# A hybrid decoder layer in split precision on one core: the low-half subtraction of four down weights made in two halves

## The chip, the core and the metric

The kernel runs on one NeuronCore of a Trainium2 chip. TensorE multiplies, VectorE, ScalarE and GpSimd do the rest of the arithmetic, and SyncE issues the DMA transfers. The metric is the device time of one execution in microseconds (us), as the median of several runs. Where the text explains where time goes, it uses one profiled execution, whose own time stands beside the median below.

## The reference

The kernel computes one decoder layer for 1024 tokens of width 1024, with 16 learned meta tokens in front, in float32. Two feed-forward networks (ffn1 and ffn2) enclose a mixer of two kinds of heads:

```python
def swiglu(h, w_gate, w_up, w_down):
    return (jax.nn.silu(h @ w_gate) * (h @ w_up)) @ w_down
...
        n = rms_norm(h, ffn1_norm[l])
        h = h + 0.5 * swiglu(n, ffn1_w_gate[l], ffn1_w_up[l], ffn1_w_down[l])
        n = rms_norm(h, mix_norm[l])
        proj = n @ w_in[l]
...
        sb_out = stick_breaking_attention(q, k, v)
        rw_out = rwkv7_time_mix(proj[..., 3 * SB_WIDTH:], ...)
        h = h + jnp.concatenate([sb_out, rw_out], axis=-1) @ w_out[l]
        n = rms_norm(h, ffn2_norm[l])
        h = h + 0.5 * swiglu(n, ffn2_w_gate[l], ffn2_w_up[l], ffn2_w_down[l])
    return rms_norm(h, final_norm)[:, N_META:]
```

The feed-forward width d_ff is 2816, which is 22 blocks of 128. The change lies in the feed-forward networks alone.

## The kernel before

**Split products.** Each float32 operand x is split into a high part, xh = round(x), and a low part, xl = x - xh. A product is three matmuls that accumulate in one PSUM bank: high by high, high by low and low by high (`mm3`, L720). A weight tile arrives by DMA as `wraw` (128 partitions by 1024 float32, 512 KB). ScalarE copies it, rounded, into `whi`; VectorE then subtracts to get `wlo`. Both are one instruction per tile (`split`, L504; `wsplit`, L558). The tiles wraw, whi and wlo have two buffers each, so a new weight can be split only when the last but one has been multiplied.

**The order of the stages.** The 1040 rows are cut into two groups, A (the meta tokens and the first half) and B (the second half). TensorE's main stream runs ffn1 on A (stage 0), the input projections of A, ffn1 on B (stage 1), the projections of B, the output projection of A, ffn2 on A (stage 2), and ffn2 on B (stage 3). Beside this main stream the mixer's work (RWKV and attention) is put into the gaps of each engine's queue. Stages 1 and 2 have mixer work beside them; in them the products of the main stream take turns in two PSUM banks (`DB = 2`, L34).

**Inside a stage.** d_ff is walked in parts (`PARTS`, L52): a first part of two blocks, then parts of four. For each block the main stream makes the gate and up products (pg, pu), and the activation is split again into `ah` and `al`. Then come the down products of the part. One part of two blocks needs two down tiles, each 2 blocks deep by 512 output columns; one of four needs four tiles. Between the up product of the last block of a part and the down products stands the gate product of the next part's first block. A down product `pd` (L1066) covers one output block m of 128, with three matmuls for each block of d_ff in the part; when it is done, VectorE adds it to the residual:

```python
            self.mm3(pd, self.row(dh, j, mw * P)[:, ms], self.row(dl, j, mw * P)[:, ms], ah, al, i == 0, i == nf - 1)
        hd = h[:, m, c0:c1]
        with self.urgent():
            nc.vector.scalar_tensor_tensor(hd, pd, 0.5, hd, ALU.mult, ALU.add)
```

The profile calls that addition `h<-pd,h`. Only it frees the PSUM bank.

**What sets the order.** Every engine works through its queue in order, and the order is fixed when the program is built. A planner (`Clock`, L195) keeps a clock for each engine with a cost per instruction (`cost`, L273). `catch_up` (L391) takes, over all engines, the pending instruction that could start first; among equals the more urgent. Loads and splits of weights have the level "load", the residual's additions are "urgent", and an urgent one is taken if it is ready no more than 0.1 after the other (`AHEAD`, L49):

```python
                    key = (max(t, c, self.port if o.port else self.dma - BACKLOG if e == "s" else 0.0)
                           - AHEAD * (o.prio[0] == -self.URGENT), o.prio)
```

`o.port` marks instructions of VectorE that read two SBUF operands, and GpSimd's: the planner lets only one of these run at a time. VectorE's cost in it is 0.11 + 0.00111 per element of a partition (L281), a matmul's of this kind 0.4545e-3 per column and 0.001 more (L300, L314). When an instruction is issued, its clock advances, and everything that follows is placed by the new state.

The weights are loaded in the order that `plan` (L1369) yields them. `loads` (L568) issues the DMA as soon as a buffer of wraw is free, `splits` (L587) calls `wsplit` for each. A small function in `plan`, `laid` (L1429), sets for each weight how its rows are laid out in the tile. In stages 1 and 2 the first block of d_ff in a down tile of two blocks lies on one side of the tile, the second on the other, 512 elements each, with a gap.

Of the kernel before, what the change touches and what calls it, by code (L numbers as in the profile page):

```python
# [7 lines left out]
F32 = mybir.dt.float32  # L8
F32R = mybir.dt.float32r
I32 = mybir.dt.int32  # L10
AF = mybir.ActivationFunctionType
ALU = mybir.AluOpType
# [53 lines left out]
def quad_order(nm):  # L66

    parts, qf = FPARTS[nm], QF[nm]
    for i, (f0, f1) in enumerate(parts):
        if f0 >= qf:  # L70
            q, nd = 0, parts[i - 1][1] - parts[i - 1][0]
            for x in "d" * nd + ("gu gu" if f1 > f0 + 2 else "gu") if f0 == qf else "gdudd gdu" if nd == 4 else "gdu gdu":
                if x == " ":
                    f0 += 2
                elif x == "d":
                    yield x, parts[i - 1], q
                    q += 1
                else:
                    yield x, None, f0
# [16 lines left out]
class Eng:  # L96


    def __init__(self, real, name, clk):
        self._r, self._n, self._c = real, name, clk  # L100
# [381 lines left out]
class Ker:  # L482
    def __init__(self, tc, A, out):
        self.tc, self.A, self.out = tc, A, out
        self.clock, self.fast = Clock(), None
        self.wq, self.wr, self.cur, self.flags = [], [], (), {}
        self.lay, self.edge = None, False
        self.nc = NC(tc.nc, self.clock)
        self.need = self.clock.need
        self.after = lambda *aps: self.clock.need(*aps, slack=False)  # L490


    def two(self, *aps, bank):

        n = self.need(*aps, bank=bank)
        n.both = True
        return n
# [57 lines left out]
        by = w.shape[3] // nm  # L555
        return w[:, k // by // 2, k // by % 2, k % by * nm:(k % by + 1) * nm]

    def wsplit(self, raw, nk, nm, pool, lay):  # L558
        self.clock.ahead = True
        self.nsplit = getattr(self, "nsplit", 0) + 1  # L560
        hi, lo = self.wtiles(nk, nm, pool, lay)
        if len(hi.shape) > 3:
            raw = raw.rearrange("p k c -> p (k c)").rearrange("p (a b c) -> p a b c", b=2, c=hi.shape[3])
        self.split(hi, lo, raw, self.nc.gpsimd if self.nsplit < 3 else None)
        self.clock.ahead = False
        return hi, lo

    def loads(self, plan):  # L568

        for x in plan:  # L570
            if not isinstance(x, tuple):
                yield x
                continue
            raws, lay = [], self.lay
            if isinstance(x[0], tuple):
                for src, ring in zip(x[0], ((self.wp, "wr", 2), (self.fast.q, "wr2", 2))):
                    yield self.need(bank=ring)
                    raws.append(self.wraw(src, *x[1:3], ring))
                    self.hold(raws[-1:])
            else:  # L580
                yield self.need(bank=(self.wp, "wr", 2))
                raws.append(self.wraw(*x[:3]))
                self.hold(raws)
            self.wr.append((x, raws, lay))
        self.wr.append(None)

    def splits(self):  # L587

        while True:
            yield lambda: self.wr  # L590
            if self.wr[0] is None:
                return
            x, raws, lay = self.wr[0]
            if len(raws) == 2:
                self.wq.append((x, []))
                yield from self.pair(raws, self.wq[-1][1])
                self.drop(raws)
                self.wr.pop(0)
                continue
            raw, = raws  # L600
            pool = self.wx if len(x) > 3 else self.wp
            for tag in ("wh", "wl"):
                yield self.need(bank=(pool, tag, 2))
            self.wq.append((x, self.wsplit(raw, *x[1:3], pool, lay)))
            self.hold(self.wq[-1][1])
            self.drop((raw,))
            self.wr.pop(0)
# [761 lines left out]
    def plan(self):  # L1369

        F = self.flags
        cols = lambda name, c0, n: (self.wcols(name)[:, :, c0:c0 + n], KT, n)

        def proj(g, late):
            rw, sb = self.proj_items(g)
            for it in 2 * sb[-NL:] if late else rw + sb[:-NL]:
                yield cols("w_in", *it[:2])

        def wout(late):
            for m in WOUT[late]:  # L1380
                yield cols("w_out", m * P, P)

        def ffn(nm, poll=False, wx=False, fast=False, once=False):
            gu = lambda c, f: cols(nm + "_w_" + c, f * P, P)
            two = lambda c, f: ((gu(c, f)[0], gu(c, f + 1)[0]), KT, P)
            kept = lambda l: [x + (True,) * (i > 1) for i, x in enumerate(l)] if wx else 2 * l
            def down(f0, f1, q):
                dw = self.A[nm + "_w_down"][0].rearrange("(f p) m -> p f m", p=P)
                mw = KT // (f1 - f0) * P
                return dw[:, f0:f1, q * mw:q * mw + mw], f1 - f0, mw  # L1390
            qf = QF.get(nm, 0)
            for f0, f1 in FPARTS[nm] if fast else PARTS:
                if fast and f0 >= qf:
                    break
                if f0 == 0 and once:
                    yield from [gu(c, f) for f in range(f0, f1) for c in ("gate", "up")]
                elif f0 == 0:
                    yield from kept([gu(c, f) for f in range(f0, f1) for c in ("gate", "up")])
                else:
                    for f in range(f0, f1):  # L1400
                        if f > f0:
                            if poll and F.get("f2b") and "woutat" not in F:
                                F["woutat"] = f
                                yield from wout(True)
                            yield gu("gate", f)
                        yield gu("up", f)
                if fast and f1 >= qf:
                    continue
                if f1 < NFT:
                    if poll and F.get("f2b") and "woutat" not in F:  # L1410
                        F["woutat"] = f1
                        yield from wout(True)
                    yield gu("gate", f1)
                self.edge = f1 == NFT and not poll
                yield from [down(f0, f1, q) for q in range(f1 - f0)]
                self.edge = False
            for op, x, f in quad_order(nm) if fast else ():
                if op == "d":
                    yield down(*x, f)
                elif op == "u" and f == NFT - 2:  # L1420
                    yield from (gu("up", f), gu("up", f + 1))
                else:
                    yield lambda: self.fast
                    yield two("gate" if op == "g" else "up", f)
            if fast:
                self.edge = True
                yield from [down(*PARTS[-1], q) for q in range(4)]
                self.edge = False
        def laid(gen, stage):  # L1429
            for x in gen:  # L1430
                if isinstance(x, tuple):
                    src = x[0][0] if isinstance(x[0], tuple) else x[0]
                    self.lay = LAY.get((0 if self.edge else stage, next((n for n in ("down", "w_out") if n in src.name), "up")))
                yield x
        yield from laid(ffn("ffn1", wx=True, fast=True), 0)
        yield from laid(proj(0, False), 0)
        yield from laid(proj(0, True), 0)
        yield from laid(ffn("ffn1", once=True), 1)
        yield from laid(proj(1, False), 1)
        yield from laid(proj(1, True), 0)  # L1440
        yield from laid(wout(False), 1)
        yield from laid(ffn("ffn2", True), 2)
        if "woutat" not in F:
            yield lambda: F.get("f2b")
            F["woutat"] = None
            yield from laid(wout(False), 2)
        yield from laid(ffn("ffn2", wx=True, fast=True), 3)
# [650 lines left out]
    def attn(self, g, bufs, nw, ahead):  # L2098
# [23 lines left out]
        def worker():  # L2122
            while items:
# [9 lines left out]
                if not any(left.values()):  # L2133
                    F["attn", g] = True
        self.clock.spawn(loads(), 4)
        self.clock.spawn(zs(), 2)
        for i in range(nw):
# [556 lines left out]
```

## Time and profile before

| | |
|---|---|
| median of 3 runs | 2219.96 us (2219.08 to 2220.79) |
| the profiled execution | 2222.34 us |
| its span, first to last instruction | 2220.6 us |
| ScalarE busy (whole span) | 1097.1 us (49%) |
| split subtractions of weights, wlo on VectorE | 312, 412.6 us in all |
| additions of a down product to the residual of A or the first stages, `h<-pd,h` | 200, 107.0 us in all |

In the profile PE is TensorE's matmuls, PEld its weight loads, DVE is VectorE, ACT ScalarE, POOL GpSimd and SPq SyncE's queue of DMA issues. A row of the timeline gives the start, the duration, the engine, the line, the operation, output and inputs (out<-in), shapes, and, in brackets, how long the engine stood idle before it and what released it. Every instruction is recorded by one helper, so all rows carry L110; they are told apart by the names of their tiles. In this execution the first part of stage 1 has its down products at 610 to 625 us and that of stage 2 at 1351 to 1364 us.

### The profile page before, as it was taken

What the parts mean: (1) busy time and instruction counts of PE and PEld (TensorE: products, weight loads), DVE (VectorE), ACT (ScalarE), POOL (GpSimd) and SP (SyncE); (2) the same over time, 40 slices, a digit from 0 to 9 for tenths busy, and PEclk for the clock granted to TensorE, in tenths of its full rate; (3) what the DMA queues carried; (4) which work ended last, traced back from release to release, by engine and by line L of the source; (5) the groups of instructions that cost most, each with busy time, mean ns of one, the idle gap of its engine ahead of it and who ended that gap; (6) DMA issues with size and microseconds to landing.
All of it is one profiled execution on the core that took longest, in us unless ns stands there. A gap on an engine that the chain in (4) does not pass through costs nothing.

```text
span 2220.6 us, 41509 instructions
## 1 busy us (share of the span) xinstructions
PE 2192.2 (99%) x16304; PEld 1954.9 (88%) x16304; DVE 1549.7 (70%) x2632; ACT 1097.1 (49%) x2177; POOL 574.1 (26%) x723
## 2 busy tenths in 40 slices
PE   9999999999999999999999999999999999999998
PEld 8999999999878888888888987887878899899998
DVE  6887776475666655576576887556777756898774
ACT  6454444534444534565435564445666436455444
POOL 2321121013142231453012424314444101322120
PEclk9999999999999999999999999999999999999999
DMA  7533332645633232432556534234232343334332
GB/s 217 147 105 105 102 89 79 174 133 137 201 106 99 76 102 77 122 97 75 160 145 191 166 102 119 73 95 129 72 90 78 117 132 121 111 105 114 105 92 80
DMA packets 408745, 257.60 MB, mean 116 GB/s; under 512 B 45013, under 2 KB 392373, under 8 KB 408550
## 3 DMA queue, kind: packets, MB, share of 16 engines
q1 hardware_dynamic: 408550, 254.95, 39.8%
q8 instruction: 128, 2.10, 0.4%
q14 instruction: 67, 0.55, 0.1%
HBM read 220.90 MB, written 33.99 MB: 115 GB/s over the span
## 4 chain that ended last, share of the span: by engine, by line
PE 91%; DVE 3%; ACT 2%; issue 2%; DMA 1%; SPq 0%; POOL 0%; DVEq 0%; ACTq 0%; POOLq 0%
PE pd L110 33%; PE pu L110 21%; PE pg L110 20%; PE pwo L110 3%; PE px L110 3%; PE po L110 2%; PE pz L110 2%; PE pat L110 2%; DVE wlo L110 1%; PE pG L110 1%; ACT whi L110 1%; SPq L110 0%; PE pp L110 0%; PE psw L110 0%; PE pss L110 0%
## 5 line engine op out<-in xcount | busy, mean ns | idle before, releaser
L110 ACT ACTIVATE whi<-wraw 128x1024 fp32r<-128x1024 f32 x314 | 330.5, 1053 | 314.4 <-PE pd L110 195.0
L110 DVE TENSOR_TENSOR wlo<-wraw,whi 128x1024 fp32r<-128x1024 f32 (+1 forms) x312 | 412.6, 1324 | 91.8 <-ACT whi L110 87.1
L110 PE MATMUL pd<-ah,whi 128*128 128x512 f32 (+2 forms) x944 | 323.1, 342 | 4.1 <-DVE h L110 3.7
L110 PE MATMUL pd<-ah,wlo 128*128 128x512 f32 (+2 forms) x944 | 317.8, 337 | 0.0
L110 PE MATMUL pd<-al,whi 128*128 128x512 f32 (+2 forms) x944 | 316.9, 336 | 0.8 <-DVE al L110 0.8
L110 PE MATMUL pd<-nh,whi 128*128 128x256 f32 (+7 forms) x648 | 210.2, 324 | 0.2 <-DVE st L110 0.2
L110 PE MATMUL pu<-nh,whi 128*128 128x512 f32 (+3 forms) x576 | 205.6, 357 | 0.0
L110 PE MATMUL pd<-nh,wlo 128*128 128x256 f32 (+7 forms) x648 | 203.9, 315 | 0.0
L110 PE MATMUL pd<-nl,whi 128*128 128x256 f32 (+7 forms) x648 | 203.5, 314 | 0.0
L110 PEld LDWEIGHTS pd<-ah,whi 128*128 128x128 f32 x944 | 177.6, 188 | 24.4 <-DVE h L110 5.0
L110 PE MATMUL pu<-nh,wlo 128*128 128x512 f32 (+3 forms) x576 | 197.2, 342 | 0.0
L110 PE MATMUL pu<-nl,whi 128*128 128x512 f32 (+3 forms) x576 | 196.1, 340 | 0.0
L110 POOL TENSOR_TENSOR qs<-wraw 128x512 f32<-128x512 f32 x64 | 98.5, 1541 | 372.0 <-DVE ql L110 141.9
L110 PE MATMUL pg<-nh,whi 128*128 128x512 f32 (+3 forms) x536 | 194.4, 364 | 0.2 <-ACT whi L110 0.2
L110 PEld LDWEIGHTS pd<-ah,wlo 128*128 128x128 f32 x944 | 177.4, 188 | 19.2
L110 PEld LDWEIGHTS pd<-al,whi 128*128 128x128 f32 x944 | 177.6, 188 | 18.2 <-DVE al L110 1.5
L110 PE MATMUL pg<-nl,whi 128*128 128x512 f32 (+3 forms) x536 | 186.2, 349 | 0.0
L110 PE MATMUL pg<-nh,wlo 128*128 128x512 f32 (+3 forms) x536 | 185.5, 351 | 0.5 <-DVE wlo L110 0.5
L110 DVE SCALAR_TENSOR_TENSOR h<-pd,h 128x256 f32<-128x256 f32 (+1 forms) x200 | 107.0, 539 | 66.9 <-PE pd L110 66.0
L110 POOL TENSOR_TENSOR al<-sl,ah 128x512 fp32r<-128x512 f32 (+2 forms) x45 | 74.3, 1651 | 297.7 <-ACT ah L110 288.2
L110 PEld LDWEIGHTS pd<-nh,whi 128*128 128x128 f32 (+2 forms) x648 | 120.8, 186 | 12.0 <-issue 3.1
L110 PEld LDWEIGHTS pd<-nh,wlo 128*128 128x128 f32 (+2 forms) x648 | 120.5, 186 | 8.3
(413 smaller groups left out, 5609.4 us busy)
## 6 DMA issues: line engine op xcount, KB each, us to landing
wraw<-in_ffn_w_gate_dram SPq DMA_DIRECT2D x90, 512.0 KB
wraw<-in_ffn_w_up_dram SPq DMA_DIRECT2D x90, 512.0 KB
wraw<-in_ffn_w_down_dram SPq DMA_DIRECT2D x88, 512.0 KB
wraw<-in_w_in_dram SPq DMA_DIRECT2D x54, 512.0 KB
wraw<-in_w_out_dram SPq DMA_DIRECT2D x20, 512.0 KB
s<-rkvd SPq DMA_DIRECT2D x18, 256.0 KB
raw<-qkvd SPq DMA_DIRECT2D x16, 264.0 KB
raw<-qkvd SPq DMA_DIRECT2D x16, 256.0 KB
```

The lines of the kernel that those rows point to most:

```text
L110: self._c.trace(self._n, op, lambda: f(*a, **k), out, [x for x in args if isinstance(x, bass.AP)], k)
```

## The change

The subtraction of a down tile that covers two blocks of d_ff, in stages 1 and 2 alone, becomes two subtractions, one for each block. These are the two down tiles of the first part in each of the two stages, four tiles in all; their highs are still made by one copy. `plan` marks such a weight (`fine`), `loads` keeps the mark with the tile, and `wsplit` acts on it:

```diff
-    def wsplit(self, raw, nk, nm, pool, lay):
+    def wsplit(self, raw, nk, nm, pool, lay, fine):
...
-        self.split(hi, lo, raw, self.nc.gpsimd if self.nsplit < 3 else None)
+        if not fine:
+            self.split(hi, lo, raw, self.nc.gpsimd if self.nsplit < 3 else None)
+        else:
+            self.nc.scalar.activation(hi, raw, AF.Copy)
+            al, m = slice(None), raw.shape[1] // 2
+            for x in ((al, slice(0, m)), (al, slice(m, 2 * m))) if m else ((al, al, 0), (al, al, 1)):
+                self.nc.vector.tensor_tensor(out=lo[x], in0=raw[x], in1=hi[x].bitcast(F32), op=ALU.subtract)
...
-            raws, lay = [], self.lay
+            raws, lay = [], (self.lay, self.fine)
...
-            self.wq.append((x, self.wsplit(raw, *x[1:3], pool, lay)))
+            self.wq.append((x, self.wsplit(raw, *x[1:3], pool, *lay)))
...
+                    self.fine = stage in (1, 2) and x[1] == 2
                     self.lay = LAY.get((0 if self.edge else stage, next((n for n in ("down", "w_out") if n in src.name), "up")))
```

With this layout the tile has the shape (128, 1, 2, 512), so m is 0 and the two halves are the two sides, `(al, al, 0)` and `(al, al, 1)`: 128x512 each. The two are separate instructions for the planner, which may put others between them.

More of the change, by code (lines that the diff above doesn't have):

```diff
@@ L486, in __init__ @@
         self.wq, self.wr, self.cur, self.flags = [], [], (), {}
-        self.lay, self.edge = None, False
+        self.lay, self.edge, self.fine = None, False, False
         self.nc = NC(tc.nc, self.clock)
```

## The prediction

> **What bounds the kernel now.** I read the page first, for the share of each engine and for the chain that ended last.
>
> ```profile
> span 2220.6 us, 41509 instructions
> ...
> PE 2192.2 (99%) x16304; PEld 1954.9 (88%) x16304; DVE 1549.7 (70%) x2632; ACT 1097.1 (49%) x2177; POOL 574.1 (26%) x723
> ...
> PE 91%; DVE 3%; ACT 2%; issue 2%; DMA 1%; SPq 0%; POOL 0%; DVEq 0%; ACTq 0%; POOLq 0%
> ```
>
> TensorE is the bound: busy 99% of the span, and 91% of the chain. VectorE, at 70%, holds the end back only where TensorE stands still for it. So the question is not how much VectorE work the change adds, but whether one of the four split subtractions lies in front of a TensorE wait. Next I read the waits of TensorE, summed by what they waited for.
>
> ```profile
> PE pd L110 <- DVE h L110: 3.7, 4, 1.4
> ```
>
> The largest group is pd (the down product) waiting for h, VectorE's addition of a finished pd to the residual. It is 3.7 us in 4 waits, the longest 1.4 us. No wait of a down product for wlo is in that list: nobody waits directly for the low halves that the change cuts. A wait for h can still be caused by a wlo, if wlo stands ahead of h in VectorE's queue. The chain of waits, in order of time, shows the place (start, duration, what):
>
> ```profile
> 1353.26 1.52 DVE rt L110
> 1354.78 1.26 DVE wlo L110
> 1356.05 0.61 DVE h L110
> ```
>
> This is the second down tile of ffn2's first part, one of the four that change. Two VectorE instructions, rt and wlo, stand ahead of an h, and the timeline shows TensorE idle behind them:
>
> ```profile
> 1353.47 1.28 POOL L110 TENSOR_TENSOR y<-y,vt 128x512 f32<-128x512 f32 x1
> ...
> 1353.59 0.39 PE L110 MATMUL pd<-ah,wlo 128*128 128x512 f32 x1
> ...
> 1354.70 1.35 DVE L110 TENSOR_TENSOR wlo<-wraw,whi 128x1024 fp32r<-128x1024 f32 x1
> 1354.72 0.25 POOL L110 TENSOR_TENSOR ltmp<-lt,T 64x39 f32<-64x39 f32 x1
> ...
> 1355.04 1.12 POOL L110 TENSOR_TENSOR T<-T,ltmp 64x39 f32<-64x39 f32 x1
> ...
> 1355.97 1.27 DVE L110 SCALAR_TENSOR_TENSOR h<-pd,h 128x512 f32<-128x512 f32 x2
> 1356.08 0.38 SPq L110 DMA_DIRECT2D wraw<-in_ffn_w_gate_dram  x1
> ...
> 1356.70 0.50 PE L110 MATMUL pd<-ah,whi 128*128 128x512 f32 x1 [1.35 <-DVE h L110]
> ...
> 1359.35 0.39 PE L110 MATMUL pd<-ah,wlo 128*128 128x512 f32 x1
> ...
> 1364.18 1.06 ACT L110 ACTIVATE whi<-wraw 128x1024 fp32r<-128x1024 f32 x1 [2.77 <-issue]
> ```
>
> The pd of output block m=1 ends at 1353.59 + 0.39 = 1353.98. Its h could run then, but VectorE is inside rt until 1354.78 and then inside wlo until 1356.05. This stage has two PSUM banks for its products, so the pd of m=3 cannot start until the h of m=1 has emptied one: 1.35 us of idle TensorE.
>
> **The change, part by part.** It removes four subtractions of 128x1024 and puts eight of 128x512 in their place, one for each block of d_ff. ScalarE's copy to whi stays whole, no DMA is added, and each half waits for the same whi, so no half adds a wait of its own. The half has a twin in the trace, the ql of a paired weight, with the same inputs, type and shape:
>
> ```profile
> L110 DVE TENSOR_TENSOR wlo<-wraw,whi x312: 873/1224/2881, 20.7 to 2197.1; 128x1024 fp32r<-128x1024 f32 x154, 128x768 fp32r<-128x768 f32 x1, 128x512 fp32r<-128x512 f32 x1
> ...
> L110 DVE TENSOR_TENSOR ql<-wraw,qh x32: 674/684/1794, 126.7 to 2156.3; 128x512 fp32r<-128x512 f32 x32
> ```
>
> Medians: 684 ns for a half, 1224 ns for a whole. Two halves cost 2 x 0.684 - 1.224 = 0.144 us more. The next VectorE instruction starts some 0.08 us before the last one ends (1354.70 + 1.35 = 1356.05 against 1355.97), so the true extra is between 0.06 and 0.14 us per tile, 0.26 to 0.58 us over four tiles, all on VectorE.
>
> *First down tile of both stages.* Cost on the path: nothing.
>
> ```profile
> 604.50 1.22 DVE L110 TENSOR_TENSOR wlo<-wraw,whi 128x1024 fp32r<-128x1024 f32 x1
> ...
> 610.80 0.39 PE L110 MATMUL pd<-ah,wlo 128*128 128x512 f32 x1
> ```
>
> ```profile
> 1344.47 1.34 DVE L110 TENSOR_TENSOR wlo<-wraw,whi 128x1024 fp32r<-128x1024 f32 x1
> ...
> 1351.54 0.40 PE L110 MATMUL pd<-ah,wlo 128*128 128x512 f32 x1
> ```
>
> The lows are ready at 605.72 and 1345.81 and first used at 610.80 and 1351.54: 5.1 and 5.7 us of cover, given by the gate product of block 2 that stands between. Even with an urgent VectorE instruction and a GpSimd instruction between the halves (0.7 and 1.3 us) the second half is in time. Without that cover the price would be the extra 0.06 to 0.14 us plus what came between.
>
> *Second down tile of stage 1* (the ffn1 pass over the second half of the sequence).
>
> ```profile
> 612.53 2.31 DVE L110 TENSOR_TENSOR wlo<-wraw,whi 128x1024 fp32r<-128x1024 f32 x1
> ...
> 614.86 0.40 SPq L110 DMA_DIRECT2D wraw<-in_ffn_w_gate_dram  x1
> ...
> 616.32 0.48 PE L110 MATMUL pd<-ah,whi 128*128 128x512 f32 x1
> ...
> 618.47 0.40 PE L110 MATMUL pd<-ah,wlo 128*128 128x512 f32 x1
> ...
> 624.95 1.06 ACT L110 ACTIVATE whi<-wraw 128x1024 fp32r<-128x1024 f32 x1 [3.37 <-issue]
> ```
>
> The same order stands here, and the h of m=1 waits behind a wlo of 2.31 us, but TensorE does not: the pd of m=3 at 616.32 carries no wait, since transposes of the mixer had been put in front of it. The low is ready at 614.84 and first used at 618.47, 3.6 us later. So nothing is won, and nothing lost.
>
> *Second down tile of stage 2.* This is where time can come. Which instruction goes between the halves is decided when the program is built: the planner takes, on each engine, the instruction that can start first by its own costs, and lets an urgent one go ahead that is ready up to 0.1 us later. h is urgent, wlo is a load. By the planner's costs (lines 281 and 301) a pd takes six matmuls of 0.234 = 1.40 and an h 0.678; so the h of m=1 is ready at most 1.40 - 0.68 = 0.72 after the h of m=0 is done, and wlo comes after that h. A half takes 0.678; with the advance, anything ready up to 0.78 after wlo's start goes between. So I expect the order half, h of m=1, half. On the chip, wlo's 1.26 us in the chain becomes one half. Its length: 0.684 - 0.08 = 0.60, plus the 0.13 by which this wlo is longer than the median (1.35 against 1.22), 0.73. Saved: 1.26 - 0.73 = 0.53 us, and the pd of m=3 starts at 1356.17.
>
> Is something else late then? The second half follows the h of m=1 and ends by about 1356.8, or 1358.1 if a GpSimd instruction of 1.28 comes ahead of it; its first reader, 1359.35 before, would stand at 1358.8. The h of m=2 ends at 1357.24 before and some 0.1 to 0.3 later after, against 1356.17 + 1.4 = 1357.6 for the pd of m=4 that needs its bank: just in time. The raw tile is given back up to 0.8 us later, so SyncE's load at 1356.08 (and that at 614.86) moves by as much, with whatever is queued behind it. The whi copies that read these two loads start at 1364.18 and 624.95, 8.1 and 10.1 us after them, so there is no loss.
>
> Bounds of this term: if both halves go after the h, all 1.26 is saved; if they stay together it costs 0.06 to 0.14; with a GpSimd instruction between, up to 1.28 + 0.14, some 1.4 us, is lost. I take 0.53, since the code's own costs lead there.
>
> [...] VectorE's rt, on 8 elements, took 1.52 us, until 1354.78, just as GpSimd's y of 1.28 ended (1354.75), and GpSimd's T of 64x39 took 1.12 while wlo ran. [...]
>
> *The rest of the program.* The planner keeps one clock for everything, so 0.1 us more on VectorE and an h that ends earlier can change the order of what follows. What that can be worth is bounded by the idle time of TensorE after the first edit:
>
> ```profile
> 604.00:1354.00 750.00, 738.48 (x5382) 620.80 (x5381) 496.67 (x904) 368.66 (x797) 233.55 (x365) 1.00 0.41 118
> 1354.00:2220.60 866.60, 854.72 (x5840) 748.34 (x5839) 624.04 (x934) 440.37 (x826) 226.60 (x202) 1.00 0.34 101
> ```
>
> The first numbers are length and TensorE's busy time: 11.52 and 11.88 us idle, 23.4 in all. A new order may close or open a part; a quarter of it, 5.9 us, is the largest I think likely, either way, and I count zero for the forecast.
>
> **Sum.** 0 + 0 + 0 - 0.53. The profiled execution took 2222.34 us (span 2220.6), so it would be 2221.8; the median of the runs, 2219.96, is 2.38 below it, so I say 2219.4. About 0.2% (4.4 us) is what a measurement of this kernel tells from no change.
>
> **Rivals.**
> 1. *Halves stay together.* The planner finds no h ready and issues both at once; the change does nothing but lengthen wlo. For: in before's order no h was ready in the plan at wlo's start. Against: the 0.72 above. Place: 1354.78; +0.06 to +0.14, 2220.1.
> [...]
> 3. *Slower by the plan.* The changed times move mixer instructions in TensorE's queue to points where their inputs are not there on the chip, although the plan thinks so. Place: after 612.53, as soon as one mixer product has changed its place in the queue relative to the FFN's, most likely in stage 1, where it had hidden the late h. Price: that stall uncovered is, by its twin in stage 2, up to 1.35 us, and a quarter of the 23.4 idle adds 5.9; from 1 us to all of it, less 0.53, is +0.5 to +6.7, middle 2223.6. For: mixer work stands at the very point. Against: TensorE's idle is only 1.4% after the edit, so most orders cost nearly nothing.
> 4. *Faster by the plan.* The same reshuffle closes waits: From 1 to 5.9 us, with the 0.53, is -1.5 to -6.4, middle 2216.0. For: 23.4 us are there to be closed. Against: each wait is short (the longest for h 1.4) and they have many causes.
>
> **How the numbers follow.** Forecast 0.45 (own range 2218.4 to 2220.4, with up to 1 us of reordering), rival 1 0.12, rival 2 0.05, rival 3 0.21, rival 4 0.17. Spread evenly over their stretches, 2.3 of 6.2 us of rival 3 lie beyond 4.4 us (0.08 of its 0.21) and 2.0 of 4.9 of rival 4 (0.07), so faster 0.07, slower 0.08, same 0.85. For 8 in 10 the range reaches into both to where a tenth is left out on each side: 2216.5 to 2223.7.
>
> **What would show it.** Eight half subtractions of about 0.68 us and four wholes fewer (VectorE 2636 instructions). In stage 2 an h between the halves, and the wait of 1.35 us near 1356 down to about 0.8. In stage 1 no wait of pd m=3 or m=4. Wrong would be: that wait as long as before (rival 1), a second half of 0.9 us or more with a GpSimd instruction beside it (rival 2), or TensorE's idle sum away from 23.4 by several us, in places far from the four tiles (rivals 3 and 4).

## The result, and the profile after

The changed kernel takes **2216.72 us** (median of 22 runs, 2213.96 to 2219.89) against 2221.08 us (22 runs, 2218.46 to 2224.78) of the kernel before, measured beside it: the ratio is 0.9978, 95% interval [0.9973, 0.9984]. It is faster by 4.4 us, 3.6 to 6.0 by the interval, which excludes no change; that is about the 0.2% that the prediction took as the least that can be told. The forecast was 2219.4, a gain of 0.5 from a median of 3 runs that lay 1.1 below the one measured here, with a range of its own that ended at 2218.4 and no measurable difference as the likeliest case. The profiled execution took 2215.46 us.

The page of the changed kernel (span; busy times; the chain that ended last):

```profile
span 2213.8 us, 41536 instructions
...
PE 2187.4 (99%) x16304; PEld 1950.2 (88%) x16304; DVE 1541.5 (70%) x2636; ACT 1097.4 (50%) x2177; POOL 570.8 (26%) x723
...
PE 92%; DVE 3%; DMA 2%; ACT 2%; issue 1%; SPq 0%; DVEq 0%; ACTq 0%
```

VectorE has the four instructions more that were forecast (2636 against 2632). Although there are more of them, its busy time fell by 8.2 us, so single instructions must have become shorter; what can lengthen one is seen further below.

In the waits of TensorE the group that led the list has shrunk from 3.7 to 1.5 us:

```profile
PE pd L110 <- DVE h L110: 1.5, 3, 0.8
```

The timeline of VectorE shows what became of the second down tile of the first part, in stage 1 and then in stage 2:

```profile
613.10 0.68 DVE L110 TENSOR_TENSOR wlo<-wraw,whi 128x512 fp32r<-128x512 f32 x1
614.26 0.69 DVE L110 SCALAR_TENSOR_TENSOR h<-pd,h 128x512 f32<-128x512 f32 x1 [0.48 <-PE pd L110]
614.87 0.68 DVE L110 TENSOR_TENSOR wlo<-wraw,whi 128x512 fp32r<-128x512 f32 x1
```

```profile
1349.03 1.03 DVE L110 TENSOR_SCALAR rt<-rt 128x8 int32<-128x8 int32 x1
1349.98 0.68 DVE L110 TENSOR_TENSOR wlo<-wraw,whi 128x512 fp32r<-128x512 f32 x1
1350.58 1.27 DVE L110 SCALAR_TENSOR_TENSOR h<-pd,h 128x512 f32<-128x512 f32 x2
1351.78 0.82 DVE L110 TENSOR_TENSOR wlo<-wraw,whi 128x512 fp32r<-128x512 f32 x1
```

The order is half, h, half in both, as forecast. In stage 2 even two additions (x2) went between. TensorE's waits there:

```profile
1351.31 0.50 PE L110 MATMUL pd<-ah,whi 128*128 128x512 f32 x1 [0.19 <-DVE h L110]
...
1356.18 0.51 PE L110 MATMUL pd<-ah,whi 128*128 128x512 f32 x1 [0.47 <-DVE h L110]
```

The wait of 1.35 us is down to 0.19, and a new one of 0.47 stands 5 us later, behind the wlo of the next weight. So at this place some 0.7 us is gone in this pair of profiles. That is not 4.4.

**Where the rest went.** The stretches of stage 1 and stage 2 in the two traces (start:end, length, then TensorE's busy time), before and after:

```profile
604.00:1093.00 489.00, 484.77 (x3313) 397.41 (x3312) 305.43 (x531) 235.32 (x512) 159.49 (x233) 1.00 0.34 98
1331.00:1787.00 456.00, 451.34 (x2895) 368.90 (x2895) 314.24 (x420) 238.54 (x456) 165.98 (x174) 1.00 0.33 97
```

```profile
604.00:1093.00 489.00, 487.07 (x3324) 399.72 (x3323) 301.48 (x534) 236.97 (x513) 158.13 (x233) 1.00 0.35 98
1331.00:1787.00 456.00, 453.08 (x2921) 371.19 (x2920) 310.31 (x423) 237.79 (x455) 163.69 (x174) 1.00 0.34 100
```

TensorE's idle time is length less busy time: 4.23 us before and 1.93 after in stage 1, 4.66 and 2.92 in stage 2. In stage 1, where the forecast had put nothing, 2.3 us of idle time went. In the kernel before, four of the five longest waits of that stage are these rows of TensorE's timeline; the fifth, 0.58 us near 1061, is in both kernels (between the first and the last of the four lie some 430 us):

```profile
622.08 0.50 PE L110 MATMUL pd<-ah,whi 128*128 128x512 f32 x1 [0.51 <-DVE h L110]
...
666.50 0.66 PE L110 MATMUL pu<-us,tt 128*128 128x64 f32 x4 [0.66 <-ACT us L110]
...
1044.53 0.39 PE L110 MATMUL pd<-ah,whi 128*128 128x256 f32 x1 [1.04 <-DVE h L110]
...
1051.15 0.39 PE L110 MATMUL pd<-ah,whi 128*128 128x256 f32 x1 [0.77 <-DVE h L110]
```

None of the four is in the trace after, and none belongs to a tile that was cut. The changed kernel has a new one of this size, two down products behind the last of them:

```profile
1052.07 0.36 PE L110 MATMUL pd<-ah,whi 128*128 128x256 f32 x1 [0.83 <-DVE h L110]
```

The four make 2.98 us, less the new 0.83 some 2.15 of the 2.3. Two of those that went can be followed row by row.

At 622 us, TensorE before had four transposes of the mixer (pyT) early, at 618.81, and then nothing to do while it waited for h. After, the transposes stand exactly at that point:

```profile
618.81 0.66 PE L110 MATMUL pyT<-ident,y 128*128 128x128 f32 x4
```

```profile
621.51 0.63 PE L110 MATMUL pyT<-ident,y 128*128 128x128 f32 x4
621.90 0.48 PE L110 MATMUL pd<-ah,whi 128*128 128x512 f32 x1
```

At 666 us, VectorE before had a whole wlo of another weight ahead of the copy us, which feeds TensorE's pu. After, the wlo of the same weight (661.65) follows the copy of the mixer's step before (661.44) and is done long before the copy of this step (667.44), whose pu has no wait. The rows before, then after:

```profile
663.50 2.33 DVE L110 TENSOR_TENSOR wlo<-wraw,whi 128x1024 fp32r<-128x1024 f32 x1
665.86 0.28 DVE L110 COPY us<-px 64x128 f32<-64x128 f32 x1
```

```profile
661.44 0.28 DVE L110 COPY us<-px 64x128 f32<-64x128 f32 x1 [0.84 <-PE px L110]
661.65 1.21 DVE L110 TENSOR_TENSOR wlo<-wraw,whi 128x1024 fp32r<-128x1024 f32 x1
...
667.44 0.28 DVE L110 COPY us<-px 64x128 f32<-64x128 f32 x1 [1.66 <-PE px L110]
```

So the time seems to have come from another order of the queues, and not from the halves. Compared instruction by instruction, TensorE's queues in the two programs agree up to the cuts in stage 1, differ in order from 613.5 to 1047.7 us (times of before), agree again up to the cuts in stage 2, differ from 1359.6 to 1740.6, and agree from there on.

### The profile page after: what moved, and what is told of

Read it like the earlier page. It is cut to its first block, busy times and chain, and to the rows that moved or that the text cites. A ratio compares the mean times of both kernels' runs of the same rounds, so it can differ in the third digit from the quotient of the medians.

```text
span 2213.8 us, 41536 instructions
## 1 busy us (share of the span) xinstructions
PE 2187.4 (99%) x16304; PEld 1950.2 (88%) x16304; DVE 1541.5 (70%) x2636; ACT 1097.4 (50%) x2177; POOL 570.8 (26%) x723
## 4 chain that ended last, share of the span: by engine, by line
PE 92%; DVE 3%; DMA 2%; ACT 2%; issue 1%; SPq 0%; DVEq 0%; ACTq 0%
PE pd L110 33%; PE pu L110 22%; PE pg L110 21%; PE pwo L110 3%; PE px L110 3%; PE po L110 2%; PE pz L110 2%; PE pat L110 2%; DVE wlo L110 1%; PE pG L110 1%; ACT whi L110 1%; DMA rkvd<-st 0%; PE psw L110 0%; PE pp L110 0%; PE pss L110 0%
## 5 line engine op out<-in xcount | busy, mean ns | idle before, releaser
L110 ACT ACTIVATE whi<-wraw 128x1024 fp32r<-128x1024 f32 x314 | 330.5, 1052 | 289.8 <-PE pd L110 185.0
L110 DVE TENSOR_TENSOR wlo<-wraw,whi 128x1024 fp32r<-128x1024 f32 (+2 forms) x316 | 402.2, 1275 | 88.9 <-ACT whi L110 82.5
```

What stands on the lines that cost most here:

```text
L110: self._c.trace(self._n, op, lambda: f(*a, **k), out, [x for x in args if isinstance(x, bass.AP)], k)
```

## The experiments

**The theories.** *Order*: the changed costs give the planner another order in stages 1 and 2, which happens to leave fewer waits; the halves themselves bring next to nothing. *Halves*: the h that runs between the halves brings the gain, directly or because everything behind it is earlier. All ratios below are to the kernel before, run on the same chip (median 2221.2 to 2221.4), with 11 runs of each timed kernel, or 10.

### The cut alone, and the order alone

e1_cut_old_order cuts the four subtractions, but the planner sees one instruction at its old cost, so that every queue keeps the order of before; the second half is put behind the next VectorE instruction:

```diff
...
+            def first():
+                sub((al, al, 0))
+                self.clock.late = (lo.name, lambda: sub((al, al, 1)))
+            self.clock.trace("v", "tensor_tensor", first, lo, [raw, hi.bitcast(F32)], dict(op=ALU.subtract))
```

> The four subtractions are cut, but the planner still sees one instruction with the old cost, so every queue keeps the order of before; the second half is put behind the one VectorE instruction that stood behind the whole (in the second down tile of both stages that is the h of m=1). Theory P (the gain is the new order of everything that follows): only the direct part is left, TensorE's wait of 1.35 us near 1357 shrinks to 0.2 to 0.8, the time falls by 0.5 to 1.3 us. Theory H (the gain comes from the halves and the earlier h themselves): the whole gain of the change, 4 to 5 us.

e2_whole_new_order is the reverse: the planner sees two halves and makes the order of the changed kernel, but where the first half stood the whole subtraction is issued, and nothing where the second stood:

```diff
...
+            def once():
+                if todo:
+                    todo.pop()
+                    self.nc.vector._r.tensor_tensor(out=lo, in0=raw, in1=hi.bitcast(F32), op=ALU.subtract)
+            for x in ((al, al, 0), (al, al, 1)):
+                self.clock.trace("v", "tensor_tensor", once, lo[x], [raw[x], hi[x].bitcast(F32)], dict(op=ALU.subtract))
```

> The reverse: the planner sees two halves and orders every queue as in the changed kernel, but where the first half stands the whole 128x1024 subtraction is issued, and where the second stands nothing. Theory P: the gain stays but for the direct part, 3 to 4.2 us faster than before. Theory H: as before, within 0.5 us.

Measured: e1 2220.71 us, ratio 1.0 [0.9991, 1.0008]; e2 2217.01 us, ratio 0.998 [0.9972, 0.9989]. TensorE, ScalarE and GpSimd have the order of before in e1 and that of the changed kernel in e2, instruction for instruction. The cut without the order brings nothing that can be measured (the 0.5 to 1.3 us that were expected of it lie inside the interval), and the order without the cut brings the whole gain. The theory of the halves falls.

In e1 stands a second half of 0.9 us or more with a GpSimd instruction beside it, the sign that the prediction's last lines give for its second rival. VectorE's second half took 1.43 us instead of 0.68, while GpSimd's y ran from 1352.84 to 1354.13:

```profile
1353.25 1.43 DVE L581 TENSOR_TENSOR wlo<-wraw,whi 128x512 fp32r<-128x512 f32 x1
```

```profile
1352.84 1.29 POOL L110 TENSOR_TENSOR y<-y,vt 128x512 f32<-128x512 f32 x1
```

The half ended at 1354.68, 0.55 us after y; the first half took 0.68. So the late half looks as if it had begun about when y ended, but its row does not say what it waited for. The product m=3 has no wait of its own any more, but the next one, m=4, waits 0.39 us, since its h stands behind this second half. That is what the late half cost here.

### One stage at a time

e3_stage1 makes the cut in stage 1 alone, e4_stage2 in stage 2 alone:

```diff
-                    self.fine = stage in (1, 2) and x[1] == 2
+                    self.fine = stage == 1 and x[1] == 2
```

> The cut in stage 1 alone. Its order is that of the changed kernel in stage 1 and that of before from stage 2 on. Theory P: faster by what the traces show between 600 and 1093 us, some 2.5 us, with the waits of TensorE near 622, 660, 667 and 1045 us gone. Theory H: nothing, since TensorE did not wait for an h in this stage's second down tile: within 0.3 us.

> The cut in stage 2 alone. Its order is that of before in stage 1 and that of the changed kernel in stage 2. Theory P: faster by what the traces show between 1332 and 1787 us, some 2.8 us, of which the wait near 1357 is 1.2 and the waits near 1412, 1446 and 1619 the rest. Theory H: 1.2 us, the wait near 1357 alone. If the two stages add, e3 and e4 together make the whole gain.

Measured: e3 2219.47 us, 0.9992 [0.9983, 1.0001]; e4 2218.15 us, 0.9989 [0.9981, 0.9998]. TensorE's idle time in stage 1 was 1.89 us in e3 and 4.22 in e4; in stage 2 it was 2.41 and 2.38. The two differences, 1.75 and 3.07 us, add to 4.8, about the 4.4 of the whole change, though each interval is 4 us wide. Stage 1 is clear: its 2.3 us of idle time go with its own order. Stage 2 is less so, since its idle time fell in e3 too, where its order was that of before.

### Other orders, without a cut

If any other order were better than the one before, the kernel before would simply have been unlucky. Four kernels keep whole subtractions and only give the planner another cost for the four tiles, which changes the order from there on. n_p110 adds 0.11, n_m110 takes 0.11 off, n_p500 adds 0.5 and n_p700 adds 0.7:

```diff
+        if fine:
+            self.clock.pend["v"][-1].cost += 0.11
```

> No cut at all: the four subtractions stay whole, and the planner is only told that each of them costs 0.11 more than before (1.357 for 1.247), which is what the two halves cost it in sum. Stage 1 gets a new order, close to that of the changed kernel (a few rows of TensorE's queue differ); stage 2 keeps that of before. Theory P (the order alone makes the time): like the cut in stage 1 alone, 1.5 to 2.5 us faster. If the cut itself is needed: as before, within 0.5 us.

> No cut; the planner is told 0.11 less for each of the four. Stage 1 keeps the order of before, stage 2 gets one that is neither that of before nor that of the changed kernel. Theory P: a time of its own, anywhere from 3 us faster to 3 us slower. If before's order was simply an unlucky one, any other is faster, by 1 to 3 us. If the cut itself is needed: as before, within 0.5 us.

> No cut; the planner is told 0.5 more for each of the four. Stage 1 gets a third order, stage 2 keeps that of before. Theory P: its own time, from 3 us faster to 3 us slower than before. Unlucky before: 1 to 3 us faster. Cut needed: within 0.5 us.

> No cut; the planner is told 0.7 more for each of the four. Both stages get orders that no other kernel here has. Theory P: its own time, from 5 us faster to 5 us slower than before. Unlucky before: 2 to 6 us faster. Cut needed: within 0.5 us.

Measured: n_p110 2220.05 us, 0.9994 [0.9985, 1.0003]; n_m110 2221.55, 1.0 [0.9991, 1.0009]; n_p500 2221.11, 0.9999 [0.999, 1.0008]; n_p700 2220.06, 0.9995 [0.9986, 1.0004]. n_p110, whose stage 1 has nearly the order of the changed kernel, has the same 1.88 us of idle time there. n_p700 closes waits in stage 1 (2.12 us idle) and opens others in stage 2, at the mixer's pu:

```profile
1387.65 0.92 PE L110 MATMUL pu<-us,tt 128*128 128x64 f32 x4 [1.55 <-ACT us L110]
...
1402.81 0.66 PE L110 MATMUL pu<-us,tt 128*128 128x64 f32 x4 [0.90 <-DVE us L110]
```

So the orders differ by what waits they leave, none of these four differs from before by more than the intervals, and the changed kernel's is the best of the five. n_p110 was expected at 1.5 to 2.5 us faster and came out at 1.4, with no gain still inside its interval. That any other order is a gain is not borne out: n_m110 and n_p500 lie at 0.1 us slower and 0.3 faster. Their intervals, about 2 us to either side, do not exclude a small one.

### The addition ahead of the whole subtraction

e5_h_first keeps order and whole subtractions of before, but in the second down tile of both stages wlo goes behind the h of m=1. It wins all that the direct step of the prediction could win:

```diff
...
+            def first():
+                if second:
+                    self.clock.late = (lo.name, sub)
+                else:
+                    sub()
```

> The order of before on every engine and whole subtractions, with one edit: in the second down tile of stages 1 and 2 the subtraction of 128x1024 stands behind the addition h of block m=1 instead of ahead of it, so that this h never waits for a wlo. Direct theory (the wlo ahead of h is what TensorE waits for in stage 2): the largest that can be won there, 1.26 us of before's chain, shows: wait of pd m=3 near 1356 gone from 1.35 to about 0.1, -0.5 to -1.3 us. Theory of the order (the gain of the changed kernel lies in the order of all that follows): since nothing else has moved, the time is before's within 1.3 us, none of the 4.4 us of the changed kernel beyond that shows, and the other waits of before (622, 659, 666, 1044, 1445 us) are still there. [...]

Measured: 2222.08 us, 1.0005 [0.9996, 1.0014]. There is no gain. The wait for the h of m=1 is gone, but the wlo that was moved back took 1.98 us, from 1355.12 to 1357.10 (GpSimd's y ran on until 1354.74 + 1.28 = 1356.02), and the product after it, m=4, waits 0.64 us instead. The row names rt, which stands behind the h of m=2 on VectorE; this h ran from 1357.03 to 1357.71, right behind the wlo:

```profile
1357.85 0.47 PE L110 MATMUL pd<-ah,whi 128*128 128x512 f32 x1 [0.64 <-DVE rt L110]
```

### The kernel before and the changed one, profiled again

b_again1 and b_again2 are the kernel before, a_again is the changed one, none of them edited.

> The kernel before, unchanged, profiled again. If the 1.52 us of rt and the wait of 1.35 us near 1356 are set by the order of the queues alone, both come again within 0.1 us, and the rest of the waits too. If they hang on where GpSimd happens to be in an execution, rt lies anywhere between 0.16 and 1.5 and the wait between 0.2 and 1.4. Granted clock in the stretch of the output projection (1204 to 1304 us): 0.97 again if the program causes it, 1.00 if it was that one execution.

> As the run before it: the kernel before, unchanged, a third profile. Repeat of rt 1.52 and wait 1.35 within 0.1 if the order sets them; rt between 0.16 and 1.5 otherwise. TensorE's waits of stage 1 (622, 666, 1044 us: 0.7 to 1.2 us over the usual interval) again if the order sets them.

> The changed kernel, unchanged, profiled again. If the order sets the gain, the waits that went (622, 666, 1044, 1412, 1618 us) are absent again and the span of stage 1 and stage 2 is again 2 to 3 us below before's in each; if the first profile was luck, the offsets against before scatter by 2 us or more.

Their times were 2221.4, 2221.79 and 2215.89 us. Stage 1 repeats to the hundredth: 4.23 and 4.24 us of idle time in the two, as in the first profile of before (4.23), and 1.92 in the changed kernel (1.93 in its first). The waits at 622, 666, 1044 and 1051 us are there in all three profiles of before, with the same length within 0.02 us, and in none of the changed kernel. The order makes them.

The wait near 1356 us, on which the prediction was built, does not repeat. In the second repeat of before:

```profile
1353.56 0.54 DVE L110 TENSOR_SCALAR rt<-rt 128x8 int32<-128x8 int32 x1
1354.01 1.21 DVE L110 TENSOR_TENSOR wlo<-wraw,whi 128x1024 fp32r<-128x1024 f32 x1
```

```profile
1352.78 1.29 POOL L110 TENSOR_TENSOR y<-y,lnx_b 128x512 f32<-128x512 f32 x1
```

```profile
1355.88 0.51 PE L110 MATMUL pd<-ah,whi 128*128 128x512 f32 x1 [0.23 <-DVE h L110]
```

With the same program, the same order and a whole wlo, the wait was 1.35, 0.89 and 0.23 us in the three profiles, and rt, on 8 elements, took 1.52, 1.20 and 0.54. Each time rt ended 0.03 or 0.04 us after a y of GpSimd (here 1353.56 + 0.54 = 1354.10 against 1352.78 + 1.29 = 1354.07). In e2 a y was within 0.10 us of its end when rt began (1350.59 + 1.29 = 1351.88), and the same rt took 0.16:

```profile
1351.78 0.16 DVE L110 TENSOR_SCALAR rt<-rt 128x8 int32<-128x8 int32 x1
```

So up to 1.36 of rt's 1.52 us (1.52 less the 0.16) went with GpSimd's y, and which y it met depends on the execution: y<-y,vt in the first profile of before, y<-y,lnx_b in the two repeats. The order of the starts does not explain it: in the repeats y had begun ahead of rt (1352.71 against 1352.84, and 1352.78 against 1353.56), in the first profile it began at 1353.47, 0.21 us after rt, and rt still ended 0.03 us behind it. What ties rt's end to y's is not shown by any run.

### Moving only the subtractions that stand in the way

What was read from the rows at 666 us can be tried by itself. e6_swaps keeps the order of before and whole subtractions, and moves three wlo of stage 1 back behind the instruction for which TensorE waits at 622, 666 and 1051 us. None of the three is one of the changed tiles. (The wlo ahead of the wait at 1044 us, which ends at 1043.27, was not moved: the next load of a weight is issued at 1043.30.)

```diff
...
+        n = {'wlo_8104': 1, 'wlo_8642': 1, 'wlo_12620': 2}.get(lo.name)
+        if n:
+            o = self.clock.pend["v"][-1]
+            f = o.call
+            o.call = lambda: setattr(self.clock, "late", [n, {hi.name, lo.name, raw.name}, f, {hi.name}])
```

> The kernel before in its own order, with whole subtractions, but three wlo of stage 1 (none of the four tiles of the change) moved back behind the addition h or the copy us for which TensorE waits: those before the waits at 622, 666 and 1051 us, which lost 0.68, 0.82 and 0.94 us in all three profiles of before. Theory that a wlo ahead of such an instruction makes the wait: all three go (below 0.2 each), stage 1 is 2.0 to 2.4 us shorter in the trace, TensorE's idle time from 604 to 1093 us falls from 4.23 to about 2.1; time -2 us (0.9991). Rival, that only a wholly other order helps and that a moved wlo is itself late: stage 1 the same within 0.5 us and new waits for wlo.

Measured: 2219.53 us, 0.9991 [0.9982, 0.9999], a gain of 1.75 us where 2 were expected. All three waits are gone. VectorE at the second of them, and stage 1 as a whole (4.23 us of idle time have become 2.42):

```profile
663.10 0.28 DVE L110 COPY us<-px 64x128 f32<-64x128 f32 x1 [1.67 <-PE px L110]
663.41 1.23 DVE L110 TENSOR_TENSOR wlo<-wraw,whi 128x1024 fp32r<-128x1024 f32 x1
```

```profile
604.00:1093.00 489.00, 486.58 (x3314) 398.98 (x3314) 303.62 (x527) 234.89 (x512) 159.16 (x233) 1.00 0.35 99
```

The wlo took 2.33 us ahead of the copy and takes 1.23 behind it: in before GpSimd's al ran beside it (663.46 to 664.74), in e6 al had ended at 662.70.

v1_after_swaps does the same in the changed kernel at the two waits for h that are left, 1052 and 1356 us; a_timed is the changed kernel beside it.

> The changed kernel, with two wlo of other weights moved back in the same way: those before the waits for h at 1052 us (1.00 lost) and 1356 us (0.64). By the same theory both go: -1.0 to -1.6 us against the changed kernel, 2215 to 2216. By the rival no difference, within 0.5 us.

> The changed kernel again, for the comparison with the run before it: 2216.7, 0.998 of before.

Measured: v1 2215.49 us, 0.9977 [0.9967, 0.9986]; a_timed 2217.14, 0.9985 [0.9976, 0.9994]. The difference of 1.65 us is in the expected direction and size, but the intervals overlap, so it is not settled. In v1 the wait at 1356 us is gone; that at 1052 us has been exchanged for a wait for the moved wlo itself:

```profile
1050.43 0.38 PE L110 MATMUL pd<-ah,wlo 128*128 128x256 f32 x1 [0.77 <-DVE wlo L110]
```

### Stage by stage

TensorE's idle time by the same two stretches of each trace (us), with the times:

| kernel | stage 1 | stage 2 | median | ratio to before |
|---|---|---|---|---|
| before, three profiles | 4.23, 4.23, 4.24 | 4.66, 3.32, 3.75 | 2221.08 | |
| changed, three profiles | 1.93, 1.92, 1.92 | 2.92, 2.42, 2.50 | 2216.72 | 0.9978 |
| e1, cut, order of before | 4.22 | 3.27 | 2220.71 | 1.0 |
| e2, whole, order of after | 1.93 | 2.14 | 2217.01 | 0.998 |
| e5, h ahead of wlo | 4.17 | 3.18 | 2222.08 | 1.0005 |
| e6, three wlo moved | 2.42 | 3.87 | 2219.53 | 0.9991 |

Stage 1 gives 2.3 us in every profile. Stage 2 gives 3.91 less 2.61 on average, 1.3 us, with a scatter of about the same size in one and the same program. Together that is 3.6 of the 4.4 us, the lower end of the interval.

These stretches do not hold quite the same work in both kernels, since the changed one is 1.9 us ahead at the end of stage 1 and 6.9 at the end of stage 2 (first profiles). So the stages were also timed between the same TensorE instructions, found by their place in its queue (those that start at 604.00 and 1093.18 us, and at 1331.05 and 1787.08, in the first profile of before). Stage 1 takes 489.16 to 489.23 us in the three profiles of before and 486.64 to 486.73 in the three of the changed kernel, 2.5 us less. Stage 2 takes 456.03, 454.46 and 454.96 against 453.25, 452.71 and 452.72, on average 2.3 us less. The sum, 4.8 us, covers the gain: it lies in the two stages whose order changed.

## Why the prediction was wrong

**First down tiles: nothing.** This held. In stage 1 the halves of 0.69 and 0.68 us stand at 605.07 and 606.28 us with an al between, in stage 2 both follow each other at 1340.80, and no down product waits for them.

**Second tile of stage 1: nothing.** This held for the tile itself. The half, h, half order came as in stage 2 and found no wait to shorten.

**Second tile of stage 2: -0.53.** The order was forecast rightly, from the planner's costs; the price was not. It rested on a wait of 1.35 us in one profile, taken as wlo's. Of the 2.79 us by which that h stood behind the h before it (1353.26 to 1356.05), 1.52 were rt's, which ended 0.03 us after GpSimd's y and has another length in each execution (1.52, 1.20, 0.54). The wait did fall on average, from 0.82 us (1.35, 0.89, 0.23) to 0.37 (0.19, 0.26, 0.65), near the forecast's 0.53; but the 0.47 us that stand 5 us later are in all three profiles of the changed kernel and in none of before, and e2, with whole subtractions, has the same wait (0.49). The prediction quoted rt's length beside GpSimd's y, but did not ask whether the wait it meant to shorten would be there the next time. By e1 the term is a gain of 0.5 us with an interval of about 2 to either side, and by e5 it is no gain above 0.9; its sign is not settled. What makes a VectorE instruction longer beside one of GpSimd, on which the 0.05 for the second rival rested, is shown by no run; the runs show a second half of 1.43 us in e1, with 0.39 us of TensorE's waiting behind it, and of 0.82 us in two profiles of the changed kernel.

**"The rest of the program … I count zero for the forecast."** This is the step that failed. The rest was worth the whole 4.4 us (e2: 4.2 without a cut, e1: 0.5 with the cut alone). That the forecast pointed the right way, to a gain, is luck: the term that it credited has not been shown to give any. Its bound, a quarter of TensorE's 23.4 us of idle time, held, and so did the mechanism of rival 4, "the same reshuffle closes waits", whose middle of 2216.0 lies 0.7 from the result (being the middle of a range from 1.5 to 6.4 us, it is that close by luck). The argument against it was that the waits are short and have many causes. In stage 1 they have few: e6 shows that three of them are the very pattern that the prediction had seen at 1354 us, a whole wlo ahead of an urgent VectorE instruction, and that moving those alone gives 1.75 us. That is not the 2.5 us of the changed kernel taken apart: e6 keeps the wait at 1044 us, and has none of 0.83 at 1052. The prediction followed one of the four waits for h in the list and left the other three (0.51, 1.04 and 0.77 us); all three lay in stage 1, and each h stood behind a whole wlo (at 1044 and 1051 us with another VectorE instruction, nl, between).

Could the sign have been known? Not from the profile before. Of five new orders one gave 4.4 us and four between none and 1.4, none of which can be told from nothing. Rival 3, slower by the plan with a chance of 0.21, was weighed above rival 4 at 0.17, and no order that was tried came out measurably slower. The mixer's moved products, which rival 3 feared would uncover a stall in stage 1, covered one there instead (pyT at 621.51), and in n_p700 uncovered two in stage 2.

**Open.** How much of stage 2's share is its order, and how much the state in which the stage begins: its idle time was 2.1 to 2.4 us also in the three kernels with the order of before in stage 2 and a new one in stage 1 (2.41 in e3, 2.30 in n_p110, 2.11 in n_p500), against 3.2 to 4.7 where stage 1's order was old too. Two of these three profiles, those of e3 and n_p500, were the fastest execution of their kernel (2216.32 and 2216.93 us), so they may be lucky ones. Nor do the two stages explain every median: by its idle time (1.89 and 2.41 us in e3, 1.88 and 2.30 in n_p110) either kernel should be as fast as the changed one, and they were 2.7 and 3.3 us slower, with intervals of about 2 us to either side. Between the stages, in the output projection, executions also differ by the clock: from 1250 to 1335 us the granted clock was 0.96, 0.96 and 0.98 in the three profiles of before, 1.00, 0.98 and 0.98 in those of the changed kernel. Since it varies in one and the same program, it is not counted as an effect of the change. Nor does the clock make the gain: over the whole execution it was 0.9969 on average in the 22 runs of the changed kernel and 0.9970 in the 107 runs of before that were made beside the experiments.

## What to carry to other kernels

Where a planner fixes the order of the queues at build time, an edit to one instruction's cost is an edit to everything behind it: build the changed order and the changed instruction apart, as e1 and e2 do, before crediting either. Follow every wait of the bounding engine back one step and look for a common pattern, here a long, patient instruction ahead of a short, urgent one; such places can be tried one by one, and traced again, since a moved instruction can be late itself: three moves in e6 closed their waits, one of the two in v1 exchanged its wait for another. Profile the same program a second time before building on one wait: those that an order makes came back to 0.02 us, the one behind rt, which ended each time with an instruction of GpSimd, ranged from 0.23 to 1.35.

## What was not expected of the hardware

A VectorE instruction on 128x8 elements took between 0.16 us (e2) and 1.52 us (before), and its row counts all of it as its duration. In the rows shown a 128x1024 subtraction took 1.21 to 2.33 us, and a 128x512 half 0.68 to 1.43; the long ones (2.33, 1.98 and 1.43) had begun beside an instruction of GpSimd (al from 663.46, y from 1354.74 and y from 1352.84). At these places the length of one row is therefore not the price of the instruction. VectorE's whole busy time was 1549.7 us in the first profile of before and 1541.5 in that of the changed kernel, which has four instructions more; in the stretches of stages 1 and 2 together it was 618.8 to 619.9 us in three profiles of before and 611.8 to 613.5 in three of the changed kernel. That instructions lengthened in this way explain the difference was not shown by itself.
